# Layer one's attention started behind its gMLP, with new places for column sums, weight sums and final sums

## The chip, the cores and the metric

One core of one Trainium2 chip. The metric is device time in microseconds (us) of one execution: the median of the runs shown.

## The reference, cut to what matters

Two layers of a trunk over 512 latent and 256 context tokens, width 1024. Each layer feeds four mixers from one projection, gates each and merges them.

```
def _layer(x, xc, c, c_ctx, tabs, ...):
    h = _rms(x, norm_w) * (1.0 + sc) + sh
    aq, ak, av, az, dq, dk, dv, dz, bf, bz, cu, cv, cz = _split_in(h @ w_in)
    o_a = _attend_blocked(qa, ka, va)
    o_d = _attend_window_sink(qd, kd, vd, kd_c, vd_c, sink)
    o_b = _fourier_mix(bf, w_fnet)
    o_c = _spatial_gate(cu, cv, w_sp, b_sp)
    y = _merge(h, (o_a, o_d, o_b, o_c), (az, dz, bz, cz), w_br, w_merge, b_merge, w_out)
    return x + gt * y

def _merge(h, outs, gates, w_br, w_merge, b_merge, w_out):
    yb = stack([o * silu(z) for o, z in zip(outs, gates)])
    y = einsum('bnrw,rwd->bnrd', yb, w_br)
    g = sigmoid(h @ w_merge + b_merge).reshape(b, n, N_BRANCH, D_MODEL)
    return sum(g * y, axis=2) @ w_out
```

The context tokens go through the same layer with the same weights. Only layer one (l = 0 in the code) updates them.

## The kernel before, in words

Activations lie transposed: 128 channels on the partitions, tokens along the free dimension (256 context, then 512 latent). Everything is float32 by three products: an operand is split into a rounded part hi and the rest lo, and a product is hi·hi + hi·lo + lo·hi (`mm3` L244 to L250, `block` L811 to L818).

**Weights** come as a stream of some 170 numbered items in layer one. An item is 128x512 (256 KB) or 128x256. SP loads it into wr (L216, three raw buffers), ACT rounds it into wh (L226), DVE subtracts it into wl (L227), and TensorE (PE) uses wh twice and wl once. wh and wl have three buffers each. Each call of `wnext` (L229 to L242) takes the next item, issues loads up to 5 items ahead and the rounding and subtraction up to 3 items ahead.

**Order.** The program is written as generators that yield costs; `drive` interleaves a main one with a filler, `mix` runs a step of a side job behind each step of a main one, and `laced` runs a step of `ada_rest` each time that a number of cost units has gone by. A step of `ada_rest` is one 256 KB load and two DVE instructions (L342); the steps compute the rest of both layers' modulation. A scheduler then fixes one static order for each engine, and each engine runs its list in order.

**Layer one** goes like this. The first norm and the first part of the modulation end at about 68 us. Then come the v projection, with the rotary steps of k and q (`Rope.finish`, L548 to L581, mostly DVE) mixed in, and the gMLP's u projection (`uproj`), with the stacks mixed in: 16 transfers ks and 4 qs on SP's queue that copy k and q into the layout for scores (L603, L590). Attention of branch A and then D runs as main generator, 24 units each of scores, softmax and values (`attention` L682, paced by PACE), with a filler: gMLP (`gmlp`), q projection, z projections, merge of branch C, the Fourier branch's projections, and the first 5 of the 8 column tiles j of branch A's merge (HELD). The last 3 run behind the attention, beside the Fourier mixing (`fnet`) and the column sums (`combos`, L770 to L802): sums and differences of blocks of h, split into hi and lo (tiles T2, T3, T4 and, in `first_sum`, T1).

These sums serve the merges of D and B (`merge_s`, L829). There the gate matrix of a pair of column tiles (j, j+4) is computed by seven block products in place of eight, each 128x384 wide, with sums of weight blocks (`prep`, L172 to L177). Items that hold a sum have a 'z' buffer as raw tile. In a pair the gates are multiplied with the branch products and added to M, the sum over the branches: for D by an accumulating transfer on POOL's queue (L842), for B, the last branch (`final`), by a DVE addition (L840). Then B splits M into hi (ACT, L870) and lo (DVE, L871) for the output projection. That, the second norm and layer two follow.

Names in the rows: s scores, p probabilities, tp and pt transposed ones, o attention's output, p_cu the u projection, v_cv the gMLP's v, gl and gc gate products, yl and yc branch products, z, x and y block products, g gates, sp the spatial product.

Of the kernel before, what the change touches and what calls it, by code (L numbers as in the profile page):

```python
# [19 lines left out]
P = 128  # L20
# [6 lines left out]
PACE = (3900, 4000)  # L27
# [4 lines left out]
ADA, ADA_S = 4800, 6500  # L32
HELD = 5
# [16 lines left out]
def hybrid_trunk(tc, xt, cv, crow, win, wst, wkv, wm, wo, wada, wadat, sm, bsp, wsp, wfn, kc, krope, kmask,  # L50
# [8 lines left out]
    with ExitStack() as es:  # L59
# [93 lines left out]
        def merged_s(l, r):  # L153
# [9 lines left out]
            for j in range(4):  # L163
# [7 lines left out]
                def prep(a11=a11, a12=a12, a21=a21, a22=a22, s1=s1):  # L171
# [3 lines left out]
                    V.tensor_sub(raws[a11], t, raws[a11])  # L175
                    V.tensor_sub(raws[a12], raws[a12], raws[a11])
                    s1.append(t)  # L177
# [52 lines left out]
        def wnext():  # L230
# [249 lines left out]
        for l in range(DEPTH):  # L480
# [50 lines left out]
            class Rope:  # L531
# [16 lines left out]
                def finish(self):  # L548
# [24 lines left out]
                    V.tensor_mul(s[:, 0, L], t[:, 0, L], sin)  # L573
                    V.tensor_mul(t[:, :, L], t[:, :, L], both(cos))
                    V.tensor_add(t[:, 1, L], t[:, 1, L], s[:, 0, L])
                    V.tensor_sub(t[:, 0, L], t[:, 0, L], s[:, 1, L])
                    y = pools["m"].tile([P, 4, NT], F32R, name=f"y{name}", tag="m")
                    for i in (1, 0):
                        A.copy(y[:, i, cs], t[:, i, cs])
                        V.tensor_sub(y[:, 2 + i, cs], t[:, i, cs], y[:, i, cs].bitcast(F32))  # L580
                    return y, cs  # L581
# [141 lines left out]
            def merge(r, first=False, final=False, ctag="mm", part=range(KT)):  # L723
                yb = YB[r]
                mlp = mq = None
                for j in part:
# [3 lines left out]
                    if not last:  # L730
                        gyc = bank(f"gc{l}{r}{j}", ctag)
# [97 lines left out]
            def merge_s(r, final=False):  # L829
                for j in range(4):  # L830
# [4 lines left out]
                    def gate(i, jj, g, yd):  # L835
# [3 lines left out]
                        if final:  # L839
# [14 lines left out]
                    V.tensor_add(g1[:, H2], y, g1[:, H2])  # L854
                    yd = yield from branch(r, j, ("o", "t"))
# [8 lines left out]
                    if final:  # L864
                        if j:
                            lq = pq.tile([P, 2, NT], F32R, name=f"ML{l}{j}", tag="q")
                        for i, jj in enumerate((j, j + 4)):
                            hi = tl(("yb", "k", "p", "k")[j], f"MH{l}{jj}", F32R)
                            lo = lq[:, i, :] if j else tl("yb", f"ML{l}{jj}", F32R)
                            A.activation(hi[:, WC], M[jj][:, WC], AF.Copy, scale=0.5)  # L870
                            V.scalar_tensor_tensor(out=lo[:, WC], in0=M[jj][:, WC], scalar=0.5,  # L871
                                                   in1=hi[:, WC].bitcast(F32), op0=ALU.mult, op1=ALU.subtract)
                            MH[jj], ML[jj] = hi, lo
# [200 lines left out]
            def laced(main, other, per):  # L1074

                bal = 0
                for x in main:
                    yield x
                    bal += x or 0
                    if bal >= per:  # L1080
                        bal -= per
# [21 lines left out]
            def stacks_a():  # L1103

                TAB.clear()
                yk = yield from rk.finish()
                if l == 0:
                    yq = yield from RQ[0].finish()
# [300 lines left out]
```

## Time and profile before

| | us |
|---|---|
| median of 3 runs | 1209.08 |
| lowest and highest run | 1208.01, 1211.55 |
| profiled execution, its own time | 1206.17 |
| its span | 1204.4 |
| PE busy | 1169.6 (97%) |
| DVE busy | 794.1 (66%) |
| ACT busy | 499.6 (41%) |
| POOL busy | 14.1 (1%) |

The span is the stretch from the first to the last instruction in the trace of one execution; 1.8 us lie around it. The profiled execution is 2.9 us below the median. The page gives busy time by engine; the views of the trace give what an engine waited for, the instructions in order of time, and busy time by stretch. PE is busy nearly all the time, so that its waits are what can be saved.

### The profile page before, as it was taken

How to read it: one execution, taken by the hardware profiler on the slowest of the kernel's cores; microseconds unless marked ns; L12 is line 12 of the kernel's file. 1: busy time of each engine (PE TensorE's matmuls, PEld its weight loads, DVE VectorE, ACT ScalarE, POOL GpSimd, SP SyncE). 2: the span in 40 equal slices, each digit the busy share in tenths (PEclk: the TensorE clock that was granted, in tenths of full speed). 3: DMA queues.
4: the chain of work that ended last, by engine and by line, in shares of the span. 5: the costliest groups of instructions: out<-in, count | busy, mean ns of one | idle time of the engine just before them, and what ended most of it. 6: DMA issues, size and time to landing. Idle time of an engine off the chain costs nothing.

```text
span 1204.4 us, 18892 instructions
## 1 busy us (share of the span) xinstructions
PE 1169.6 (97%) x7068; PEld 999.9 (83%) x7068; DVE 794.1 (66%) x1688; ACT 499.6 (41%) x991; POOL 14.1 (1%) x20
## 2 busy tenths in 40 slices
PE   6999999999999999799999999999999999999998
PEld 3789788888888888799898888887888888888887
DVE  5683557767767657877786469758766676454553
ACT  5443634333333423444444256545444443333431
POOL 0000000000000000010000000000000000000000
PEclk9999999999999999999999999999999999999999
DMA  8718114222222353365432444473433223333353
GB/s 319 239 29 221 49 45 105 88 71 89 94 90 81 82 155 84 97 147 150 106 123 88 133 155 141 133 200 104 121 98 103 81 85 92 88 92 96 97 170 123
DMA packets 77099, 140.38 MB, mean 117 GB/s; under 512 B 9168, under 2 KB 19536, under 8 KB 77008
## 3 DMA queue, kind: packets, MB, share of 16 engines
q1 hardware_dynamic: 66496, 119.77, 33.4%
q10 hardware_dynamic: 8208, 13.12, 3.5%
q0 software_dynamic: 2304, 6.29, 3.0%
q8 instruction: 55, 0.90, 0.3%
q14 instruction: 36, 0.29, 0.1%
HBM read 117.13 MB, written 4.19 MB: 101 GB/s over the span
## 4 chain that ended last, share of the span: by engine, by line
PE 88%; DVE 5%; DMA 3%; ACT 2%; issue 1%; SPq 1%; ACTq 0%; DVEq 0%
PE gl L247 7%; PE gl L250 7%; PE gl L248 7%; PE o L708 4%; PE tp L675 3%; PE ow L247 3%; PE ow L248 3%; PE ow L250 3%; PE p L247 3%; PE p L248 3%; PE p L250 3%; PE yl L250 2%; PE yl L247 2%; PE yl L248 2%; PE z L815 2%; PE z L817 2%
## 5 line engine op out<-in xcount | busy, mean ns | idle before, releaser
L226 ACT CAST wh<-wr 128x512 fp32r<-128x512 f32 (+1 forms) x336 | 194.2, 579 | 376.7 <-PE gl L248 89.3
L227 DVE TENSOR_TENSOR wl<-wr,wh 128x512 fp32r<-128x512 f32 (+1 forms) x336 | 213.6, 638 | 168.9 <-ACT wh L226 167.5
L247 PE MATMUL gl<-hh,wh 128*128 128x512 f32 x384 | 154.1, 401 | 0.0
L250 PE MATMUL gl<-hh,wl 128*128 128x512 f32 x384 | 150.3, 391 | 1.7 <-DVE wl L227 1.7
L248 PE MATMUL gl<-hl,wh 128*128 128x512 f32 x384 | 149.9, 390 | 0.0
L659 ACT ACTIVATE p<-s,ng 128x768 f32<-128x768 f32 (+3 forms) x80 | 60.0, 751 | 107.3 <-DVE ng L656 58.0
L651 DVE TENSOR_REDUCE mx<-s 128x1 f32<-128x768 f32 (+3 forms) x80 | 61.5, 769 | 50.5 <-PE s L645 29.3
L250 PEld LDWEIGHTS gl<-hh,wl 128*128 128x128 f32 x384 | 72.1, 188 | 17.9 <-DVE wl L227 2.1
L342 DVE CUSTOM_DVE_ANT_0 aj<-at,cb 128x512 f32<-128x512 f32 x112 | 76.0, 686 | 16.4 <-DMA at<-in_wadat_dram 14.4
L247 PEld LDWEIGHTS gl<-hh,wh 128*128 128x128 f32 x384 | 72.3, 188 | 12.9 <-ACT g L746 0.2
L248 PEld LDWEIGHTS gl<-hl,wh 128*128 128x128 f32 x384 | 72.4, 189 | 12.6
L247 PE MATMUL p<-hh,wh 128*128 128x512 f32 (+1 forms) x192 | 71.6, 373 | 0.5 <-ACT vg L910 0.5
L247 PE MATMUL ow<-MH,wh 128*128 128x512 f32 (+1 forms) x200 | 69.4, 347 | 1.0 <-DVE ones1b L404 1.0
L250 PE MATMUL ow<-MH,wl 128*128 128x512 f32 (+1 forms) x200 | 69.4, 347 | 0.8 <-DVE wl L227 0.8
L248 PE MATMUL ow<-ML,wh 128*128 128x512 f32 (+1 forms) x200 | 69.4, 347 | 0.0
L250 PE MATMUL p<-hh,wl 128*128 128x512 f32 (+1 forms) x192 | 68.2, 355 | 0.0
L248 PE MATMUL p<-hl,wh 128*128 128x512 f32 (+1 forms) x192 | 68.2, 355 | 0.0
L708 PEld LDWEIGHTS o<-pt,vt 128*64 128x64 f32 x736 | 40.8, 136 | 16.8 <-issue 13.7
L675 PEld LDWEIGHTS tp<-kconst,p 128*128 128x128 f32 x368 | 44.6, 140 | 11.0 <-issue 0.9
L675 PE MATMUL tp<-kconst,p 128*128 128x128 f32 x368 | 53.5, 273 | 0.0
L708 PE MATMUL o<-pt,vt 128*64 128x128 f32 x736 | 52.4, 279 | 0.6 <-DVE pt L677 0.6
L677 DVE COPY pt<-tp 128x384 f32<-128x384 f32 (+1 forms) x80 | 41.9, 524 | 8.9 <-PE tp L675 8.9
(532 smaller groups left out, 2772.1 us busy)
## 6 DMA issues: line engine op xcount, KB each, us to landing
wr<-in_wm_dram SPq DMA_DIRECT2D x128, 256.0 KB, 2.7
wr<-in_win_dram SPq DMA_DIRECT2D x72, 256.0 KB, 2.8
at<-in_wadat_dram SPq DMA_DIRECT2D x64, 256.0 KB, 2.7
wr<-in_wo_dram SPq DMA_DIRECT2D x40, 256.0 KB, 2.8
aw<-in_wada_dram SPq DMA_DIRECT2D x16, 512.0 KB, 5.6
wr<-in_wm_dram SPq DMA_DIRECT2D x64, 128.0 KB, 2.2
ks<-yk SPq DMA_DIRECT2D x32, 192.0 KB, 4.4
M<-g POOLq DMA_DIRECT2D x16, 384.0 KB, 4.5
```

Source lines behind the costliest of these rows:

```text
L226: A.copy(hi[:, :n], raw)
L227: V.tensor_sub(lo[:, :n], raw, hi[:, :n].bitcast(F32))
L247: T.matmul(d, wh, xh[:, c0:c1], start=first and op, stop=False)
L248: T.matmul(d, wh, xl[:, c0:c1], start=False, stop=False)
L250: T.matmul(d, wl, xh[:, c0:c1], start=False, stop=last and cl)
L342: V.tensor_tensor_reduce(out=junk[:, :512], in0=row[i], in1=cb[v], scale=0.5, scalar=0.0, op0=ALU.mult, op1=ALU.add, accum_out=macc[j // 1 ...
L651: V.reduce_max(out=mx, in_=sv, axis=AX.X)
L659: A.activation(p[:, :nk], sv, AF.Exp, bias=ng, scale=0.125, accum_out=sm_)
L675: T.transpose(tp[:, (i - g0) * P:(i - g0 + 1) * P], p[:, i * P:(i + 1) * P], ident)
L677: V.tensor_copy(pt[:, g0 * P:g1 * P], tp[:, :(g1 - g0) * P])
L708: T.matmul(dst[64 * hx:64 * hx + 64, :], vt[kt_ // 3][:, kt_ % 3, c0:c0 + 64], pts[hx][:, j * P:(j + 1) * P], start=(j == 0), stop=(j == l ...
L815: T.matmul(dst, wh[:, q], xh, start=start and i == 0, stop=False, skip_group_check=True)
```

## The change

1. Layer one's attention starts when the gMLP is done: `uproj` takes steps of the rotary finish and stacks and no longer waits for their end ("u"), and `gmlp` takes the rest ("stk"). The v projection takes a side step only every second time, and `Rope.finish` yields in more places in layer one (fine). PACE of layer one goes from 3900 to 3600.
2. All 8 column tiles of branch A's merge belong to the filler. What is left of the filler when attention ends is the main generator, with `fnet` and `combos` as its side, unscaled. `tail` runs what is left of the side, and `first_sum`, in front of the last branch product of that merge.
3. `prep` is cut in two, prep1 and prep2, at two items; sums are made up to three items ahead, behind the splits of the items in front of them, and loads of items that have sums are issued up to 9 items ahead (AHEAD).
4. In the last block merge, pairs 0 to 2 add to M by POOL's transfers, six more than before, and their split into hi and lo (`finish`) is placed in the next pair. Pair 3 stays as it was.
5. Steps of `ada_rest` come every 3900 units until attention ends (4800 before) and every 7500 in the block merges (6500 before).

PE's matmuls are the same and of the same number. Layer two is not changed.

The diff, cut:

```
-PACE = (3900, 4000)
+PACE = (3600, 4000)
-ADA, ADA_S = 4800, 6500
-HELD = 5
+ADA, ADA_S = 3900, 7500
+AHEAD = 9
...
-                item(a12, 512)
-                item(a12, 512, prep, lambda k=a11: raws[k])
+                item(a12, 512, prep1)
+                item(a12, 512, prep2, lambda k=a11: raws[k])
...
-            wload(max(k for k, *_ in items[i:i + LOADS]))
-            wround(i + 2)
-            while prepped[0] < min(i + 3, len(items)):
+            wload(max(it[0] for n, it in enumerate(items[i:i + AHEAD]) if n < LOADS or it[2]))
+            wround(i + 3)
+            while prepped[0] < min(i + 4, len(items)):
...
-            wround(i + 3)
...
+                    if tail and j == KT - 1:
+                        tail()
                     wh, wl = wnext()
                     yield from mmp(yd, wh, wl, yb, 0, 2)
...
-                        if final:
+                        if final and j == 3:
                             V.tensor_add(M[jj][:, WC], M[jj][:, WC], g[:, WC])
                         else:
                             G.dma_start(M[jj], g, accum_op=ALU.add)
...
                     A.copy(g1[:, H2], z)
                     V.tensor_add(g1[:, H2], y, g1[:, H2])
+                    if final and j:
+                        finish(j - 1)
...
-                pre = [("v", lambda: mix(vproj("v", list(range(6)), vsink), sa, False))]
+                pre = [("v", lambda: mix(vproj("v", list(range(6)), vsink), sa, False, 2))]
...
-                pre += [("stk", lambda: mix(uproj(), sa)), ("gmlp", gmlp)]
+                pre += [("u", lambda: mix(uproj(), sa, False)), ("stk", lambda: mix(gmlp(), sa))]
...
-                ("ma", ("a0", lambda: laced(merge(R_A, part=range(own)), ada, ADA))),
+                ("ma", ("a0", lambda: laced(merge(R_A, tail=tail), ada, rate))),
...
             drive(att(), filler)
-            run(filler)
             if l == 0:
-                side = seq([("fnet", fnet), ("sums", combos)])
-                drive(paced(merge(R_A, ctag="o", part=range(own, KT)), 1.0), side)
-                run(side)
-                first_sum()
+                drive(filler, side)
```

**Three places in the engines' lists.** Line numbers in rows of the change are its own, some 2 to 24 higher than before's.

DVE behind the attention, where the column sums lie: fa and fb are sums of h's tiles, T2l, T3l and T4l parts of the sums' lo, wl a weight item's lo. Before, a stretch between two wl:

```order
L786 TENSOR_TENSOR fa_5180<-hh_1_186,hl_1_194 128x768
L227 TENSOR_TENSOR wl_5218<-wr_5144,wh_5217 128x512
L788 TENSOR_TENSOR T_5116<-fa_5180 128x384
L786 TENSOR_TENSOR fa_5224<-hh_2_187,hl_2_195 128x768
L789 TENSOR_TENSOR fa_5180<-fb_5181,fa_5180 128x384
L788 TENSOR_TENSOR T_5117<-fa_5224 128x384
L790 TENSOR_TENSOR fb_5181<-fb_5181,T_5116 128x384
L796 TENSOR_TENSOR T3l_5112<-fa_5180,T3h_5110 128x384
L791 TENSOR_TENSOR fb_5181<-fb_5181 128x384
L789 TENSOR_TENSOR fa_5224<-fb_5225,fa_5224 128x384
```

And now, the end of the first of two such stretches (28 rows lie between the wl ahead of it and the one below), in the same place of the work:

```order
L801 TENSOR_TENSOR fb_4941<-fb_4941,T_4938 128x384
L799 TENSOR_TENSOR T_4938<-fa_4984 128x384
L802 TENSOR_TENSOR fb_4941<-fb_4941 128x384
L807 TENSOR_TENSOR T2l_4930<-fb_4941,T2h_4928 128x384
L800 TENSOR_TENSOR fa_4984<-fb_4985,fa_4984 128x384
L807 TENSOR_TENSOR T3l_4934<-fa_4940,T3h_4932 128x384
L807 TENSOR_TENSOR T4l_4937<-fb_4941,T4h_4936 128x384
L801 TENSOR_TENSOR fb_4985<-fb_4985,T_4938 128x384
L807 TENSOR_TENSOR T3l_4934<-fa_4984,T3h_4932 128x384
L802 TENSOR_TENSOR fb_4985<-fb_4985 128x384
L807 TENSOR_TENSOR T2l_4930<-fb_4985,T2h_4928 128x384
L229 TENSOR_TENSOR wl_5013<-wr_4842,wh_5012 128x512
```

The sums' rows have moved from a stretch with 11 rows between two wl to two stretches with more, 28 and then, over three items, 30.

ACT in the last block merge, behind the first pair: wh is a weight item's rounding, MH the hi of the final sum, g the gates, z a block product. Before, then now:

```order
L870 ACTIVATE MH_6393<-M_2193 128x768
L861 ACTIVATE g_6200<-g_6200,bmh_683 128x768
L226 CAST wh_6411<-wr_6304 128x512
L226 CAST wh_6436<-wr_6322 128x512
L870 ACTIVATE MH_6397<-M_2890 128x768
L226 CAST wh_6454<-s_114_6406 128x512
L845 COPY g_6404<-z_6401 128x384
L848 ACTIVATE g_6404<-g_6404,bmh_683 128x384
```

```order
L885 ACTIVATE g_6248<-g_6248,bmh_683 128x768
L228 CAST wh_6434<-wr_6288 128x512
L847 ACTIVATE MH_6532<-M_2193 128x768
L228 CAST wh_6453<-wr_6290 128x512
L867 COPY g_6432<-z_6429 128x384
L228 CAST wh_6481<-s_114_6389 128x512
L847 ACTIVATE MH_6536<-M_2920 128x768
L870 ACTIVATE g_6432<-g_6432,bmh_683 128x384
L228 CAST wh_6498<-wr_6451 128x256
L872 COPY g_6433<-z_6429 128x384
```

Each MH has moved back by two to three rows, behind the next pair's first copy in the second case.

PE where attention starts: s are the first scores. Before, they stood among the gMLP's v products (the row of o is attention's):

```order
L524 MATMUL v_cv_4_1113<-wh_1116,hl_5_198 128x256
L521 MATMUL v_cv_0_1111<-wh_1173,hh_6_191 128x256
L523 MATMUL v_cv_0_1111<-wl_1174,hh_6_191 128x256
L524 MATMUL v_cv_0_1111<-wh_1173,hl_6_199 128x256
L708 MATMUL o_1320<-pt_1216,vt_0_706 64x128
```

And now:

```order
L942 MATMUL sp_1428<-wsp_1288,vg_1110 64x128 x8
L942 MATMUL sp_1438<-wsp_1288,vg_1110 64x128 x4
L640 MATMUL s_1483<-ks_975,qs_1063 128x256
L641 MATMUL s_1483<-ks_984,qs_1063 128x256
L942 MATMUL sp_1450<-wsp_1288,vg_1110 64x128 x8
L942 MATMUL sp_1460<-wsp_1288,vg_1110 64x128 x4
L653 MATMUL s_1483<-ks_975,qs_1063 128x512
L654 MATMUL s_1483<-ks_984,qs_1063 128x512
L248 MATMUL p_q_1472<-hh_0_185,wh_1362 128x512
```

The first scores have moved behind the v products and z projection of the gMLP, to its spatial product; the q projection follows them.

## Rows read from the trace of the kernel before

**Rows 1.** Page, part 1: busy time, share of span, instructions, by engine.
```profile
PE 1169.6 (97%) x7068; PEld 999.9 (83%) x7068; DVE 794.1 (66%) x1688; ACT 499.6 (41%) x991; POOL 14.1 (1%) x20
```

**Rows 2.** Waits of PE over the span: us in total, times, longest.
```profile
PE z L815 <- ACT wh L226: 5.5, 2, 3.6
PE s L631 <- ACT p L659: 2.7, 4, 1.0
PE gl L250 <- DVE wl L227: 1.7, 1, 1.7
...
PE z L815 <- ACT g L845: 1.4, 1, 1.4
PE gc L247 <- DVE g L748: 1.4, 1, 1.4
...
PE p_cu L247 <- ACT vt L885: 0.8, 1, 0.8
...
PE p_cu L247 <- ACT wh L226: 0.6, 1, 0.6
PE o L708 <- DVE pt L677: 0.6, 1, 0.6
PE p L247 <- ACT vg L910: 0.5, 1, 0.5
```

**Rows 3.** Windows: length, then PE, PEld, DVE, ACT, POOL busy (x), PEclk, DMA share, GB/s.
```profile
480.00:500.00 20.00, 13.73 (x78) 11.74 (x76) 19.59 (x37) 11.16 (x22) 1.72 (x2) 1.00 0.36 79
...
502.00:503.00 1.00, 1.00 (x4) 1.00 (x4) 0.28 (x1) 0.00 (x0) 0.00 (x0) 0.50 0.80 252
```

**Rows 4.** Timeline of PE, 498 to 506: start, duration, engine, line, operation [idle <-releaser].
```profile
500.40 0.44 PE L815 MATMUL z<-T2h,wh 128*128 128x384 f32 x1 [3.62 <-ACT wh L226]
500.69 0.34 PE L816 MATMUL z<-T2l,wh 128*128 128x384 f32 x1
...
501.42 0.52 PE L815 MATMUL z<-T2h,wh 128*128 128x384 f32 x1
501.74 0.52 PE L816 MATMUL z<-T2l,wh 128*128 128x384 f32 x1
...
505.23 0.33 PE L816 MATMUL y<-T3l,wh 128*128 128x384 f32 x1
505.40 0.33 PE L817 MATMUL y<-T3h,wl 128*128 128x384 f32 x1
```

**Rows 5.** Timeline of PE, 413 to 418: a context query of attention.
```profile
415.89 0.39 PE L631 MATMUL s<-ks,qs 128*128 128x256 f32 x1 [1.03 <-ACT p L659]
```

**Rows 6.** Groups by line and form, DVE: count | busy us, mean ns.
```profile
L796 DVE TENSOR_TENSOR T2l<-fb,T2h 128x384 fp32r<-128x384 f32 x4 | 2.2, 557 | 0.1
```

**Rows 7.** Page, part 5: costliest groups, count | busy us, mean ns.
```profile
L342 DVE CUSTOM_DVE_ANT_0 aj<-at,cb 128x512 f32<-128x512 f32 x112 | 76.0, 686 | 16.4 <-DMA at<-in_wadat_dram 14.4
```

**Rows 8.** Timeline of DVE, 625 to 640, in the final merge.
```profile
634.21 0.96 DVE L840 TENSOR_TENSOR M<-M,g 128x768 f32<-128x768 f32 x1
...
638.95 1.29 DVE L227 TENSOR_TENSOR wl<-wr,wh 128x512 fp32r<-128x512 f32 x2
```

**Rows 9.** Tile M: the accumulating transfers of the merge (durations ns).
```profile
L842 POOL DMA_DIRECT2D M<-g x8: 859/859/862, 515.2 to 575.1; - x8
...
DMA to landing us min/median/max: 3.9/4.5/5.2
```

**Rows 10.** Timeline of POOL and ACT, 515 to 525, second block merge.
```profile
518.60 0.86 POOL L842 DMA_DIRECT2D M<-g  x1 [2.58 <-DVE g L837]
...
522.10 0.62 ACT L848 ACTIVATE g<-g,bmh 128x384 f32<-128x384 f32 x1 [0.20 <-DVE g L847]
```

**Rows 11.** Timeline of SP, ACT and PE behind the stack transfers, 100 to 120.
```profile
111.61 7.51 SPq L216 DMA_DIRECT2D wr<-in_win_dram  x4
...
117.42 0.62 ACT L226 CAST wh<-wr 128x512 fp32r<-128x512 f32 x1 [1.22 <-DMA wr<-in_win_dram]
...
119.38 0.28 PE L521 MATMUL v_cv<-wh,hh 128*128 128x256 f32 x1
```

More of the change, by code (lines that the diff above doesn't have):

```diff
@@ L546, in take, with finish @@
                                         op0=ALU.mult)
-                def finish(self):
+                def finish(self, fine=False):
                     cs, name = self.cs, self.name
@@ L721, in hybrid_trunk, with merge @@
             MH, ML = [None] * KT, [None] * KT
-            def merge(r, first=False, final=False, ctag="mm", part=range(KT)):
+            def merge(r, first=False, final=False, ctag="mm", tail=None):
                 yb = YB[r]
                 mlp = mq = None
-                for j in part:
+                for j in range(KT):
                     g_l = bank(f"gl{l}{r}{j}")
@@ L730, in merge @@
                     if not last:
-                        gyc = bank(f"gc{l}{r}{j}", ctag)
+                        gyc = bank(f"gc{l}{r}{j}", "o" if "a1" in flags else ctag)
                         gd.append((gyc[:, :NC], 0, NC, True, False))
@@ L829, in merge_s, with finish @@
             def merge_s(r, final=False):
+                def finish(j):
+                    if j:
+                        lq = pq.tile([P, 2, NT], F32R, name=f"ML{l}{j}", tag="q")
+                    for i, jj in enumerate((j, j + 4)):
+                        hi = tl(("yb", "k", "p", "k")[j], f"MH{l}{jj}", F32R)
+                        lo = lq[:, i, :] if j else tl("yb", f"ML{l}{jj}", F32R)
+                        A.activation(hi[:, WC], M[jj][:, WC], AF.Copy, scale=0.5)
+                        V.scalar_tensor_tensor(out=lo[:, WC], in0=M[jj][:, WC], scalar=0.5,
+                                               in1=hi[:, WC].bitcast(F32), op0=ALU.mult, op1=ALU.subtract)
+                        MH[jj], ML[jj] = hi, lo
                 for j in range(4):
@@ L863, in merge_s @@
                     gate(1, j + 4, g1, yd)
[L864 to L873, printed above, removed]
+                    if final and j == 3:
+                        finish(j)
             KS, Q = {0: [], 1: []}, {0: [], 1: []}
@@ L1079, in laced @@
                     bal += x or 0
-                    if bal >= per:
-                        bal -= per
+                    p = per[0] if "a1" not in flags else per[1]
+                    if bal >= p:
+                        bal -= p
                         next(other, None)
@@ L1105, in stacks_a @@
                 TAB.clear()
-                yk = yield from rk.finish()
+                yk = yield from rk.finish(l == 0)
                 if l == 0:
-                    yq = yield from RQ[0].finish()
+                    yq = yield from RQ[0].finish(True)
                 while ("u" if l else "v") not in flags:
@@ L1135, in hybrid_trunk, with tail @@
                 ada = ada_rest([(1, j) for j in range(16, 24)], 1)
-            own = HELD if l == 0 else KT
+            if l == 0:
+                side = seq([("fnet", fnet), ("sums", combos)])
+                def tail():
+                    run(side)
+                    first_sum()
+            else:
+                tail = None
             filler = seq(pre + [
                 ("q1", lambda: qblock(1)), ("z0", lambda: mix(zblock(0), sd)),
-                ("mc", lambda: laced(merge(R_C, first=True), ada, ADA)), ("z1", lambda: laced(zblock(1), ada, ADA)),
-                ("b", lambda: laced(bproj(), ada, ADA)),
-                ("ma", ("a0", lambda: laced(merge(R_A, part=range(own)), ada, ADA))),
+                ("mc", lambda: laced(merge(R_C, first=True), ada, rate)), ("z1", lambda: laced(zblock(1), ada, rate)),
+                ("b", lambda: laced(bproj(), ada, rate)),
+                ("ma", ("a0", lambda: laced(merge(R_A, tail=tail), ada, rate))),
             ])
-            pace = PACE[l]
+            pace, rate = PACE[l], (ADA, ADA_S)
             def att():
```

20 lines of the change are left out of this document (15 added, 5 removed).

## The prediction

> **What bounds the kernel now.** First the page: PE is busy 1169.6 of 1204.4 us [rows 1], so everything that any rearrangement can win lies in the other 34.8. Then the view of PE's waits [rows 2]. It tells what ended each wait, and the reader is to see that no single one is large: the rows are a list of short waits, nine kinds in layer one, 15.2 us in all. Two groups are in the first part: four waits of scores for the previous probabilities (2.7), two of the u projection (0.8 and 0.6), one each of attention's output (0.6) and of a projection for the gMLP (0.5). The others lie around the column sums and in the block merges: 1.7 and 1.4 for DVE's rows of branch A's merge, 5.5 in two for a rounded weight, 1.4 for a gate copy. Third, the windows [rows 3]: from 480 to 500 us DVE is busy 19.59 of 20 us and PE only 13.73, so there DVE is the bound. Fourth, PE's timeline behind it [rows 4]: after the wait of 3.62 us matmuls of 384 columns start every 0.32 us (501.42, 501.74), and at 505.23 and 505.40 every 0.17. The granted clock is 0.50 between [rows 3], the lower level of 1.2 GHz. It lasts for some 12 matmuls, 501.4 to 505.0, and so costs about 12 x 0.15 = 1.8 us. With it the most that the change can reach is 15.2 + 1.8 = 17 us.
>
> **The change, part by part**, as gains (+) and losses (-) of time.
>
> *Rotary finish spread over more steps.* The u projection's second weight stands behind a long row of DVE work, and its bank waits for ACT. With the finer steps the weight's lo is due in between: both waits go, +1.4 [rows 2]. What is late next is the weight behind the 20 stack transfers: SP's queue comes to it at 111.61, and it is rounded at 117.42 [rows 11]. Before, attention's first units lay ahead of its use, 1.8 us of matmuls (three scores of 0.7 and 0.4 for transposes, less what now lies there too) and 1.4 of waits that are gone. So PE wants it 3.2 us earlier than 119.38, the first use before [rows 11], at 116.2, and with rounding it is there at 118.0. If SP's transfers start no earlier, the loss is 1.8; the key's part is now finished before the query's and lets SP start sooner, which makes it nothing. I take the middle, -0.9, and keep 0 to -1.8.
>
> *Attention behind the gMLP.* Its first units no longer share ACT with GELU, whose table loads stand between the exponentials. Of the waits there, output and projection (0.6 + 0.5) and two of the four of scores go: +2.1. The other two are context queries, the 1.03 of [rows 5] and one like it of 0.66: a short unit that follows another after only 1.85 us of PE's work. In the new order at least 3.8 us lie between: +1.7. Against it, the rotary finish of the second query, some 12 us of DVE between two weights, now lies among full units with 768 keys. The trace has no such place; bounds are nothing and three waits as long as the longest of scores, 1.0 [rows 2]. I take one: -1.0. The spatial product, for which scores are now queued in front, waits for a bank that DVE releases behind a weight: nothing to -1.0, nearest to the 0.5 for a projection [rows 2]; -0.5.
>
> *Column sums right behind attention.* This is the largest loss. In DVE's new list 28 rows and one weight's lo lie between the last Fourier product and the third item behind it. Of these 13 are 128x384 of 0.56 [rows 6], three are 128x768 of 0.96 [rows 8], the rest are ten short ones, two of 0.42, and the weight. That is 14.2 us, 11.5 with the 0.09 by which neighbours overlap (two weights take 1.29 and not 1.38, [rows 8]). PE has matmuls for 8.5 us in that stretch, counted in its list at the pitch of 0.17 us for 384 columns [rows 4], others by their columns. Over the next three items it is 15 of 128x384, three of 128x768, four steps of the modulation of 0.69 [rows 7], and weights and gates: 16.9, less overlap 14.4, against 11.0 of PE. PE waits 3.0 and 3.4, with a little for latencies 6.6. The waits of 1.7 and 1.4 that the same work costs now [rows 2] end: -3.5. Bounds: no more than now (0), and without overlap (-8.4). I take the middle value since DVE's rows between 480 and 500 run that closely [rows 3].
>
> *Sums three items ahead, first pair of the block merges.* The wait of 3.62 [rows 4] is for sums whose last load waits for a buffer, then lands, is summed four times and rounded. Loading and two sums come earlier now, the buffer does not: 2.7 are left, +0.9 (0 to +3.6).
>
> *Last block merge.* Two waits, 1.9 (5.5 less 3.6) and 1.4 [rows 2], follow runs of DVE of seven and more us in which additions to M and splits of 0.96 [rows 8] stand ahead of weights. Six additions leave DVE, some 14 steps of the modulation go to earlier places, and splits and weight sums alternate with the weights: +3.3. The price is a new wait: ACT's MH now needs a transfer's landing, and rounded weights and copies of the next pair are queued behind it. The template is the merge before: the second transfer is issued at 518.60 [rows 10], lands 3.9 to 5.2 later [rows 9], at 522.5 to 523.8, and ACT's gate, which is now behind MH, starts at 522.10 there. With MH's own 0.9 ACT falls back 1.3 to 2.6 us. Three weight buffers of 12 matmuls each are 2 x 12 x 0.17 = 4.1 us ahead at this place, less 1.2 for rounding and lo: PE does not see it. I take off 0.3 and keep 0 to -1: +3.0. POOL, with 14.1 us of work in all, is not a bound.
>
> Of these transfers the Trainium skill (SBUF — State Buffer, "SBUF: two separate sides") has a rule against the change: their descriptors are written by GpSimd, which a DVE instruction with the shared port locks out, so that a short transfer took five times as long. Here no run shows that: POOL's eight issues take 859 to 862 ns each beside a busy DVE [rows 9]. By the row the part gives +3.0; what the rule would make of it is the third rival.
>
> *Each wait* also costs at its end: the first matmuls start 0.29 apart and not 0.17 [rows 4]. Some ten go and three come: 7 x 0.12 = +0.8. *The clock* falls once before and, I assume, once after: 0.
>
> *Sum:* 1.4 - 0.9 + 2.1 + 1.7 - 1.0 - 0.5 - 3.5 + 0.9 + 3.0 + 0.8 = +4.0. The span becomes 1200.4 and the profiled execution 1202.2. That execution is 2.9 below the median of 1209.1, so the forecast for the median is **1205.1 us**.
>
> **The rivals.** (A) *The column sums cost no more than they do now.* If weights are far enough ahead when the Fourier products end, DVE's excess of 3.0 and 3.4 is mostly taken by the lead. For it speaks that a full DVE cost only 3.1 in the present place, against it that the new stretch puts 26 us of DVE beside 19.5 of PE. That gives back 3.5, and without a wait as long as 3.6 the clock does not fall: 1.8 more. 1205.1 - 5.3 = 1199.8.
>
> (B) *They cost the clock too.* Both new waits come near the 3.62 behind which the clock fell. Two more falls: 1205.1 + 3.6 = 1208.7, no change.
>
> (C) *The transfers land late,* the slower side. Place: MH in the last merge's pairs 1 to 3. An accumulating transfer beside DVE's uninterrupted run (as the additions and weights of [rows 8] are part of) waits for it. From a landing of about 8 us on (5.2 and the 2.9 of lead) each pair stalls by the excess; at 11 us, three pairs by 3 us: 1205.1 + 9 = 1214. It makes the change slower than before from 9.4 us on. Against it speaks that no transfer of M landed later than 5.2 [rows 9]. The Trainium skill's rule, above, would do just this.
>
> (D) *The start of attention does not get better.* It is only moved: the waits for probabilities and tables come back at the new place (2.1 and 1.7 not won, two more waits of 1.0). 1205.1 + 5.8 = 1210.9.
>
> **How the numbers follow.** A measurement of this kernel tells 0.3%, 3.6 us, from no change; the line is 1205.5. Chances: forecast 0.42, A 0.22, B 0.16, C 0.08, D 0.12. The forecast's own range is 1202 to 1208.5, with a little more than half under the line. Faster: 0.24 + 0.22 + a little of B, 0.48. Slower, over 1212.7: most of C and a third of D and the worst of the column sums, 0.16. No change: 0.36. The range from 1199 to 1211.5 leaves out C and the ends of A and D.
>
> **What would show it.** In the changed kernel's profile the waits of u projection, scores behind probabilities and gates in the last merge are gone from PE's list; the wait for lo behind DVE's column sums is there twice with 3 us or so, each at DVE over 95% busy; the first block product still waits 2 to 3 us; MH on ACT shows a wait for the transfer of 1 to 2 us that nothing on PE answers to. I am wrong if PE waits less than 3 us around the column sums (A), if the granted clock falls more than once behind 400 us (B), if matmuls of the last merge wait for weights rounded behind MH (C), or if the attention's first ten units show waits over 3 us in all (D).

## The result, and the profile after

| | median us | lowest and highest | ratio to before |
|---|---|---|---|
| before | 1208.93 (4 runs) | 1208.01, 1211.55 | |
| the change | 1200.13 (4 runs) | 1198.33, 1201.62 | 0.9923 (0.9901 to 0.9945) |

The change makes the kernel 0.8% faster, 8.8 us by the medians, where 4.0 were forecast. The forecast of 1205.1 us is 5 us too slow; the time lies in the stated range, near its lower end. Its profiled execution took 1201.11 us, with a span of 1199.3.

First the waits of PE (us in total, times, longest), now a shorter list around the change, some rows left out:

```profile
PE gl L251 <- DVE wl L229: 4.0, 2, 3.5
PE z L826 <- DVE wr L179: 3.2, 1, 3.2
...
PE n1b L412 <- DVE nq1b L391: 1.4, 1, 1.4
...
PE yl L248 <- ACT g L757: 0.6, 1, 0.6
PE gcs L995 <- DMA kd<-in_kdft_dram: 0.6, 1, 0.6
PE z L826 <- ACT g L872: 0.3, 2, 0.2
...
PE v_cv L524 <- DVE wl L229: 0.2, 1, 0.2
```

Against [rows 2]: scores behind probabilities (2.7), the u projection's two waits (0.8 and 0.6), attention's output (0.6) and the gMLP's projection (0.5) are gone. Of the block merges' waits the two late ones are gone but for 0.3, the wait of the first block product is 3.2 and not 3.6, and DVE's column sums cost 4.0 and 0.6 where they cost 1.7 and 1.4. The wait of n1b, in the second norm behind layer one, is not the change's alone: it is 0.8, 1.0 and 0.3 in three kernels below (e4, e3, e10) that hold only parts of it.

Then the windows around the sums and the first block product (length, then PE, PEld, DVE, ACT, POOL busy (x), PEclk, DMA share, GB/s), to be read against [rows 3]:

```profile
440.00:445.00 5.00, 2.24 (x10) 1.50 (x8) 5.00 (x11) 2.81 (x6) 0.00 (x0) 0.93 0.11 41
445.00:452.00 7.00, 6.25 (x22) 5.12 (x23) 6.69 (x15) 1.74 (x4) 0.86 (x1) 0.57 0.58 142
...
496.00:503.00 7.00, 6.58 (x22) 6.57 (x23) 4.47 (x10) 2.21 (x5) 0.00 (x0) 0.55 0.27 79
```

The granted clock lies at 0.57 and 0.55 in two stretches of 7 us. Window by window it is 0.50 from 445 to 451 and from 496 to 502, the lower level of 1.2 GHz (the half clock, below), and it fell while PE waited. Before, there was one such stretch of some 3.4 us [rows 3, 4].

PE's timeline of the same place (start, duration, engine, line, operation [idle <-releaser]) and DVE's beside it:

```profile
441.85 0.39 PE L249 MATMUL gl<-hl,wh 128*128 128x512 f32 x1
445.75 0.80 PE L251 MATMUL gl<-hh,wl 128*128 128x512 f32 x1 [3.51 <-DVE wl L229]
446.34 0.63 PE L248 MATMUL gl<-hh,wh 128*128 128x512 f32 x1
446.77 0.63 PE L249 MATMUL gl<-hl,wh 128*128 128x512 f32 x1
```

```profile
432.97 0.68 DVE L229 TENSOR_TENSOR wl<-wr,wh 128x512 fp32r<-128x512 f32 x1
...
443.61 0.55 DVE L807 TENSOR_TENSOR T3l<-fa,T3h 128x384 fp32r<-128x384 f32 x1
444.08 0.55 DVE L802 TENSOR_TENSOR fb<-fb 128x384 f32<-128x384 f32 x1
444.55 0.55 DVE L807 TENSOR_TENSOR T2l<-fb,T2h 128x384 fp32r<-128x384 f32 x1
445.01 0.68 DVE L229 TENSOR_TENSOR wl<-wr,wh 128x512 fp32r<-128x512 f32 x1
```

DVE runs without a pause from 433.94 to 446; between the two wl (432.97 and 445.01) lie just the 28 rows that the changed list showed, and PE, which needs the second, stands from 442.2 to 445.75. Behind it, matmuls of 512 columns start 0.43 to 0.59 apart, 0.23 being usual.

Third, ACT's timeline in the last block merge, behind a transfer that POOL issued at 590.67, and then the tile M with its groups of issues and landings:

```profile
595.62 0.85 ACT L847 ACTIVATE MH<-M 128x768 fp32r<-128x768 f32 x1 [1.77 <-DMA M<-g]
596.37 0.60 ACT L870 ACTIVATE g<-g,bmh 128x384 f32<-128x384 f32 x1
...
597.18 0.47 ACT L872 COPY g<-z 128x384 f32<-128x384 f32 x1
```

```profile
L864 POOL DMA_DIRECT2D M<-g x14: 859/860/862, 511.9 to 629.2; - x14
...
DMA to landing us min/median/max: 3.9/4.7/5.8
```

MH stands behind the transfer for 1.77 us (0.75 to 1.77 in the six places; forecast 1 to 2). The landing row is of all transfers of M; the 14 of the block merges took 3.9 to 5.7, the six new ones 3.9 to 4.9. All that PE shows of it is the 0.3 of z behind ACT's copy.

### The profile page after: what moved, and what is told of

It reads as the page before. It is cut to its first block, busy times and chain, and to the rows that moved or that the text cites. A ratio compares the mean times of both kernels' runs of the same rounds, so it can differ in the third digit from the quotient of the medians.

```text
span 1199.3 us, 18917 instructions
## 1 busy us (share of the span) xinstructions
PE 1168.8 (97%) x7068; PEld 1002.9 (84%) x7068; DVE 788.2 (66%) x1682; ACT 495.7 (41%) x987; POOL 19.3 (2%) x26
## 4 chain that ended last, share of the span: by engine, by line
PE 81%; DMA 8%; DVE 7%; issue 2%; ACT 1%; SPq 1%; ACTq 0%; DVEq 0%; POOLq 0%
PE gl L248 7%; PE gl L251 7%; PE gl L249 7%; PE o L717 4%; PE tp L684 3%; PE ow L248 3%; PE ow L249 3%; PE ow L251 3%; PE p L248 2%; PE yl L251 2%; PE yl L248 2%; PE yl L249 2%; PE p L251 2%; PE p L249 2%; DMA at<-in_wadat_dram 2%
## 5 line engine op out<-in xcount | busy, mean ns | idle before, releaser
L686 DVE COPY pt<-tp 128x384 f32<-128x384 f32 (+1 forms) x80 | 41.9, 523 | 10.1 <-PE tp L684 9.7
```

The source lines that it names most:

```text
L686: V.tensor_copy(pt[:, g0 * P:g1 * P], tp[:, :(g1 - g0) * P])
```

## The experiments

All ratios are to the kernel before, in runs on the same chip, with 95% intervals. Three batches of four ran; before's median was 1208.07, 1207.85 and 1208.63 us in them. Where a kernel is said to be faster or slower than before by some us, it is the ratio's distance from 1 times 1208. One kernel against another goes by the medians; the change ran in a batch of its own, in which before was 1208.93, so that against the change the ratios give up to 2 us less of a gain.

### The kernel before, again (e1_before)

No edit.

> The kernel before, once more. Its recorded execution took 1206.2 us, its timed runs 1208.0 to 1211.6. Theory: the same waits, 1208.5 to 1209.5 us; the waits around the column sums and in front of the first block product come out a little longer than in the recorded execution, and the half clock (granted 0.50) lasts some 7 us behind them and not 3.4, which is 1.8 us more. Rival: no more half clock than in the record; then the 2.7 us between record and runs lie in waits elsewhere, or in no place that the views show.

Measured: 1208.11 us (1206.81 to 1210.82, 11 runs), ratio 1.0000 (0.9991 to 1.0008). Behind 66 us the waits of 0.8 us and more are those of [rows 2], but the half clock is found in a second place, behind the u projection's two waits. PE's timeline and the window there:

```profile
88.05 0.38 PE L247 MATMUL p_cu<-hh,wh 128*128 128x256 f32 x1 [0.84 <-ACT vt L885]
...
89.11 0.50 PE L247 MATMUL p_cu<-hh,wh 128*128 128x512 f32 x1 [0.56 <-ACT wh L226]
...
91.09 0.63 PE L250 MATMUL p_cu<-hh,wl 128*128 128x512 f32 x1
91.51 0.63 PE L247 MATMUL p_cu<-hh,wh 128*128 128x512 f32 x1
```

```profile
91.00:92.00 1.00, 1.00 (x4) 0.72 (x3) 1.00 (x2) 0.00 (x0) 0.00 (x0) 0.50 0.99 368
```

From 90 to 93.6 matmuls of 512 columns start 0.43 us apart. The same stretch stands in the run of the last merge alone (e3_final, 88 to 92) and in that of e11_behind (90 to 93). It is not in the execution that the prediction was made from, nor in that of e4_sums:

```profile
88.00:93.00 5.00, 4.94 (x25) 4.00 (x26) 5.00 (x8) 1.85 (x4) 0.00 (x0) 1.00 0.98 276
```

Two short waits of 0.84 and 0.56, with 0.5 us of work between, are so followed by the half clock in three executions of five that have them. The half clock behind the first block product is there in both, 3.4 us long, so the expectation of a longer one failed. In these 11 runs the clock does not sort the times: those with a mean clock of 0.999 took 1207.9 to 1209.4, those with 0.997 1206.8 to 1209.0. Over the 66 runs of this kernel in the three batches it does in part: 18 with 0.999 took 1207.3 us on average, 33 with 0.997 took 1208.5, and each of the two groups spreads over 4 us.

### The attention part alone (e2_attention)

```
-PACE = (3900, 4000)
+PACE = (3600, 4000)
...
-                pre = [("v", lambda: mix(vproj("v", list(range(6)), vsink), sa, False))]
+                pre = [("v", lambda: mix(vproj("v", list(range(6)), vsink), sa, False, 2))]
...
-                pre += [("stk", lambda: mix(uproj(), sa)), ("gmlp", gmlp)]
+                pre += [("u", lambda: mix(uproj(), sa, False)), ("stk", lambda: mix(gmlp(), sa))]
```

and the finer steps of `Rope.finish`, all on the kernel before.

> Only the attention part of the change on the kernel before: rotary finish in finer steps, start behind the gMLP, pace 3600. Theory (waits end one by one): the waits of the u projection (1.4 us), of output, projection and scores at attention's start (2.1) and of the two context queries (1.7) are gone, 0.3 comes back at the gMLP's v, column sums and merges stay as before: 5 to 6 us faster, about 1203.5. Rival (the parts help each other): the column sums, which then meet another place in attention's end, take 2 us or more of it back: 1205 or more.

Measured: 1197.50 us (1196.99 to 1198.22, 4 runs), ratio 0.9909 (0.9895 to 0.9922). This part alone is 11 us faster than before, twice what was expected. Its median is 2.6 below that of the whole change, with overlapping intervals. PE's waits in layer one are now, but for 0.3 of attention's output, only those of the sums and merges, unchanged:

```profile
PE z L823 <- ACT wh L226: 5.5, 2, 3.6
...
PE gl L250 <- DVE wl L227: 1.7, 1, 1.7
PE z L823 <- ACT g L853: 1.4, 1, 1.4
PE gc L247 <- DVE g L756: 1.4, 1, 1.4
```

Where the 9.8 us between the spans of e1 and e2 (1205.0 and 1195.2) lie can be read from the starts of the same matmuls: the first of the u projection (p_cu) and the first of the gMLP's v (v_cv), in e1 and then in e2.

```profile
86.57 0.40 PE L247 MATMUL p_cu<-hh,wh 128*128 128x512 f32 x1
107.09 0.28 PE L521 MATMUL v_cv<-wh,hh 128*128 128x256 f32 x1
```

```profile
86.03 0.40 PE L247 MATMUL p_cu<-hh,wh 128*128 128x512 f32 x1
102.75 0.28 PE L521 MATMUL v_cv<-wh,hh 128*128 128x256 f32 x1
```

- Up to the v projection e2 gets 0.5 us ahead, where no edit lies, and keeps this up to the u projection.
- The 96 matmuls of the u projection take 20.5 us in e1 and 16.7 in e2. Before and e4_sums, which have its two waits without the half clock, take 18.9 each. So the two waits of 1.4 cost 2.2 with their ends, and the half clock 1.6.
- From v_cv to the first z it is 387.9 us in e1 and 381.6 in e2, 6.3 less. Nearly all of it lies in attention's own matmuls: s, tp and o, from each start to the next, take 78.0 and 71.9. Of the 6.3, 2.6 are waits in the list. What sets the other 3.7 stays open.
- Behind the first z, where no edit lies, 0.8 are lost again.

### Its two halves (e10_fine, e11_behind)

e10_fine: the finer steps of `Rope.finish` and

```
-                pre = [("v", lambda: mix(vproj("v", list(range(6)), vsink), sa, False))]
+                pre = [("v", lambda: mix(vproj("v", list(range(6)), vsink), sa, False, 2))]
```

> Only the finer steps of the rotary finish (and a side step behind every second step of the v projection) on the kernel before; attention starts where it did. Theory: the two waits of the u projection (1.4 us) go, and the half clock of 3.4 us that follows them in some executions (1.8 us) with them: 2 to 3.5 us faster, 1204.5 to 1206. Rival: the wait only moves to the weight behind the stack transfers; less than 1 us faster.

Measured: 1204.73 us (1201.58 to 1208.04, 12 runs), ratio 0.9974 (0.9963 to 0.9985). The u projection's waits are gone, and no half clock stands before 500 us: the theory. In the traces the u projection takes 16.7 us, 3.8 less than in e1, and from v_cv to the first z nothing changes (387.9 both). How much of the 3.1 is the clock's is not shown by the runs: their mean clock is 0.9975, that of the 17 runs of before beside them 0.9974.

e11_behind: the order alone.

```
-                pre += [("stk", lambda: mix(uproj(), sa)), ("gmlp", gmlp)]
+                pre += [("u", lambda: mix(uproj(), sa, False)), ("stk", lambda: mix(gmlp(), sa))]
```

> Only the start of attention behind the gMLP on the kernel before; the rotary finish and the pace stay as they were. Theory: the waits at attention's start (2.1 us) and of the two context queries (1.7) go, those of the u projection and the half clock behind stay: 4 to 7 us faster, 1201 to 1204; with the finer steps it makes up the 10.6 us of the attention part. Rival: the order counts for less than the waits that end, and most of the 10.6 us needs both together: 2 us or less faster.

Measured: 1203.81 us (1202.56 to 1204.05, 5 runs), ratio 0.9960 (0.9947 to 0.9972). All four waits of scores are gone, and with them those of output and projection; the u projection keeps its 0.84 and 0.56 and the half clock behind. So the context queries' waits did end with the new order and not with the pace. From v_cv to the first z it takes 382.7 us, 5.2 less than e1. The halves make 3.1 and 4.8, 7.9 of the 11; in the traces, from the u projection to the first z, 3.8 and 5.2 of the 10.1 of e2. What the rest needs, the pace of 3600 or both together, was not tried.

### The last block merge alone (e3_final)

```
-                        if final:
+                        if final and j == 3:
                             V.tensor_add(M[jj][:, WC], M[jj][:, WC], g[:, WC])
...
                     V.tensor_add(g1[:, H2], y, g1[:, H2])
+                    if final and j:
+                        finish(j - 1)
```

> Only the last block merge of the change on the kernel before: additions to M by transfers in pairs 0 to 2, splits in the next pair. Theory: two of the three waits of that merge go (1.4 and 1.9 us), no new one comes, since landing takes 3.9 to 5.8 us and ACT's MH waits 1 to 2 us beside weights that are far enough ahead: 3 to 4 us faster, about 1205.5. Rival (transfers late): MH holds up the rounded weights, PE waits in three pairs: no faster, 1208 or more. Second rival: without the weight sums' new places a part of the waits stays: 1 to 2 us faster.

Measured: 1206.28 us (1204.52 to 1208.26, 11 runs), ratio 0.9981 (0.9972 to 0.9990): 2.3 us faster, between the theory and its second rival. PE's waits of 1.9 and 1.4 are gone, and two of 1.1 together have come:

```profile
PE z L815 <- ACT wh L226: 3.6, 1, 3.6
...
PE z L815 <- ACT g L861: 1.1, 2, 0.6
```

It is the new wait that the prediction priced at 0.3. ACT's timeline at its second place shows how it comes about:

```profile
601.20 0.85 ACT L836 ACTIVATE MH<-M 128x768 fp32r<-128x768 f32 x1 [2.50 <-DMA M<-g]
...
602.75 0.47 ACT L861 COPY g<-z 128x384 f32<-128x384 f32 x1
603.12 0.62 ACT L226 CAST wh<-wr 128x512 fp32r<-128x512 f32 x1
```

MH waits 2.50 us for the transfer, and the copy of z behind it ends at 603.2; PE, which needs z's bank for the next product, has been idle for almost 0.6 by then. A transfer's landing so does reach PE, by a copy and not by the rounded weights, and by 0.6 in a pair, not by 3.

### The column sums' place alone (e4_sums)

```
-                for j in part:
+                for j in range(KT):
...
+                    if tail and j == KT - 1:
+                        tail()
...
             drive(att(), filler)
-            run(filler)
             if l == 0:
-                side = seq([("fnet", fnet), ("sums", combos)])
-                drive(paced(merge(R_A, ctag="o", part=range(own, KT)), 1.0), side)
-                run(side)
-                first_sum()
+                drive(filler, side)
```

> Only the new place of the column sums on the kernel before: all of branch A's merge in the filler, the sums right behind attention. Theory: DVE has runs of 17 and 6 us between two weights' lo there, so the wait on PE is longer than in the changed kernel (some 5 to 8 us in place of 3.1), with one or two half clocks of 7 us, and the wait for the first block product is 3: slower by 3 to 6 us, 1212 to 1215. Rival: the place itself brings the gain (weights ahead, first block product not held up): 1 to 3 us faster.

Measured: 1211.39 us (1210.23 to 1215.64, 11 runs), ratio 1.0032 (1.0022 to 1.0042): slower by 3.9. The waits that grew:

```profile
PE gl L246 <- ACT g L747: 5.2, 1, 5.2
PE z L816 <- DVE wr L175: 3.3, 1, 3.3
```

ACT's gates, which must empty the banks, come late:

```profile
455.45 0.47 ACT L747 ACTIVATE g<-gc,bmh 128x256 f32<-128x256 f32 x1 [7.75 <-DVE macc L341]
455.87 0.51 ACT L796 CAST T2h<-fb 128x384 fp32r<-128x384 f32 x1
456.29 0.68 ACT L747 ACTIVATE g<-gl,bmh 128x512 f32<-128x512 f32 x1
```

The first has stood for 7.75 us behind DVE, which runs without a pause from 449.63 on, and one rounding of the sums lies between it and the second, for which PE waits. The granted clock is 0.50 for 6 us behind each of PE's two waits. So this part of the change loses time, by its waits and by the clock.

### The change without it, without the weight sums' order, and with the old rates (e8_oldsums, e9_oldprep, e12_ada)

e8_oldsums is the change with the edit of e4_sums undone.

> The change without its new place for the column sums: the last three column tiles of branch A's merge stand behind attention again, with the sums beside them. Theory (the parts add): the attention part gave 10.6, the last merge 1.8, the sums' place lost 3.3, so this is about 3 us faster than the change, 1196 to 1198, with waits of 1.7, 1.4 and 3.6 at the sums and one half clock of 3.4 us. Rival (the sums' place pays in company with the other parts): slower than the change, 1201 or more.

Measured: 1196.45 us (1195.10 to 1199.80, 6 runs), ratio 0.9909 (0.9893 to 0.9926). The waits are the expected ones (1.7, 1.4, and 3.7), the half clock one of 3.4 us. The median is the expected one, 3.7 below the change (1.7 by the ratios); the two intervals overlap (0.9901 to 0.9945 for the change), so that the loss of the sums' place stands on e4_sums.

e9_oldprep is the change with this undone:

```
-                item(a12, 512, prep1)
-                item(a12, 512, prep2, lambda k=a11: raws[k])
+                item(a12, 512)
+                item(a12, 512, prep, lambda k=a11: raws[k])
...
-            wload(max(it[0] for n, it in enumerate(items[i:i + AHEAD]) if n < LOADS or it[2]))
-            wround(i + 3)
-            while prepped[0] < min(i + 4, len(items)):
+            wload(max(k for k, *_ in items[i:i + LOADS]))
+            wround(i + 2)
+            while prepped[0] < min(i + 3, len(items)):
...
+            wround(i + 3)
```

> The change with the weight blocks' sums as before: in one piece, made right before their first item, no loads ahead. Theory: in the last merge a wait or two comes back (up to 2 us, as in the run of the last merge alone, which kept 1.1 us behind ACT's copies), the first block product waits 3.2 to 3.6 as it does now: 0 to 2.5 us slower than the change. Rival: DVE has room in those merges, so nothing changes, within 0.5 us.

Measured: 1201.85 us (1200.59 to 1202.96, 6 runs), ratio 0.9945 (0.9932 to 0.9958). The median lies 1.7 above the change (2.7 by the ratios), the intervals overlap, and no wait of the merges came back: the first block product waits 3.1, and the last merge 0.2. A gain of this part is not shown.

e12_ada is the change with `ADA, ADA_S = 4800, 6500`.

> The change with the steps of the modulation at their old rates, 4800 and 6500. Theory: DVE has less to do beside the column sums (four steps of 0.69 us fewer in the second run), and more in the last merge; the sums' second wait (1.1 us) goes, the first (3.5) stays: within 1 us of the change, rather faster. Rival: the steps in the last merge bring its waits back: 1 to 3 us slower.

Measured: 1199.51 us (1198.17 to 1201.21, 6 runs), ratio 0.9926 (0.9914 to 0.9938): no difference to the change. Inside, a wait of 1.4 is back in the last merge and 3.9 stands at the sums.

### The sums spread, the weight block's buffer, and both (e5_spread, e6_raw, e7_both)

e5_spread, on the change:

```
-                drive(filler, side)
+                drive(paced(filler, 0.6), side)
```

> The change, with the column sums and Fourier steps spread: behind attention the costs of branch A's merge count 0.6, so that the side job takes about 1.7 times as much of PE's work. DVE's longest run between two weights' lo falls from some 12 us to some 6. Theory (the crowding of DVE there is what costs): the waits of 3.5, 0.5 and 0.6 us around the sums and the half clock of 6.8 us behind the first of them (2.6 us) go, those of the first block product (3.2) and the half clock behind it stay: 5 to 7 us faster than the change, about 1194. Rival (the sums cost DVE the same wherever they lie): the waits are only cut in smaller pieces, less than 2 us faster.

Measured: 1190.94 us (1189.54 to 1193.11, 4 runs), ratio 0.9861 (0.9844 to 0.9878), 9.2 us below the change by the medians, 7.5 by the ratios, whose intervals do not overlap. The windows around the sums:

```profile
440.00:460.00 20.00, 20.00 (x117) 17.68 (x116) 19.44 (x44) 9.57 (x19) 1.72 (x2) 1.00 0.58 145
460.00:480.00 20.00, 20.00 (x116) 17.37 (x115) 15.52 (x36) 8.88 (x17) 1.72 (x2) 1.00 0.52 126
```

From 440 to 460 DVE is as busy as in the change (19.44 and 19.55 us), but PE now is 20.00 (15.89 in the change) and its clock 1.00 (0.83). So what cost time was not the amount of DVE's work but the 28 rows between two weights. The longest time from one wl to the next beside the sums, which was 12.0 us, now is 7.0:

```profile
432.61 0.69 DVE L229 TENSOR_TENSOR wl<-wr,wh 128x512 fp32r<-128x512 f32 x1
439.59 0.69 DVE L229 TENSOR_TENSOR wl<-wr,wh 128x512 fp32r<-128x512 f32 x1
```

Up to the output projection this execution is 8.9 us ahead of the change's. Of this 4.6 are waits; 2.7 are the half clock behind them, which is gone (half of 5.3 us of work); and 1.2 the one at the first block product, which is 3.4 us long here and not 6.8, though the wait in front of it (3.2) is the same. Against it stands a wait of 1.7 us for the Fourier matrix kd, which was 0.6. That makes 7.4; where the other 1.5 come from is not shown.

e6_raw, on the change:

```
-                return (wm[l, r, j, :, 512 * h:512 * h + 512], 512, "wraw" if h and j < 4 else "z")
+                return (wm[l, r, j, :, 512 * h:512 * h + 512], 512,
+                        "wraw" if h and j < 4 else "p" if h and j == 4 and r == R_D else "z")
```

with `wload` taking the tile from the pool that is named.

> The change, with the one weight block of the first pair that its first sum waits for (wr86) in a buffer of the pool p in place of z, where it had to wait for the split of the Fourier branch's output. Theory: its load is issued some items earlier, the wait of 3.2 us in front of the first block product goes to under 1 us, and with it the half clock behind (2.8 us): 4 to 6 us faster than the change. Rival: the load is then held by another buffer or by SP's queue, and the wait stays: within 1 us of the change.

Measured: 1195.75 us (1192.85 to 1202.52, 6 runs), ratio 0.9904 (0.9881 to 0.9926). The wait in front of the first block product is gone from PE's list. The profiled execution, the slowest of the six (1202.52), has another in its place:

```profile
PE gl L252 <- DVE wl L230: 4.0, 2, 3.5
...
PE gcs L996 <- DMA kd<-in_kdft_dram: 2.6, 1, 2.6
```

The Fourier matrix kd lands only when it is needed, in the change and in its variants with the sums' new place: this wait is 0.6 to 2.6 us there, and before has none. Here a half clock came with it, and another at 48 us, in the modulation; layer one's v projection starts 2.7 us later than in the change. From the first z to the output projection this execution takes 151.6 us, the change 157.5. The median is 4.4 below the change (2.3 by the ratios), with overlapping intervals: the mechanism is shown, the gain is not separated from noise.

e7_both is the two edits together.

> Spread sums and the other buffer together. Theory: both gains add, no half clock is left behind 400 us: 9 to 12 us faster than the change, about 1190, and faster than the attention part alone. Rival: the spread sums end later and hold up the first block product, so that the second gain is lost: 1194 or more.

Measured: 1189.07 us (1186.12 to 1190.43, 4 runs), ratio 0.9841 (0.9822 to 0.9859), the fastest of all, 19 us below before and 11 below the change (10 by the ratios). From e5_spread it isn't told apart. Its windows between 440 and 500:

```profile
440.00:460.00 20.00, 20.00 (x116) 17.64 (x115) 19.44 (x44) 9.57 (x20) 1.72 (x2) 1.00 0.58 146
460.00:480.00 20.00, 19.52 (x111) 16.81 (x110) 16.42 (x37) 7.98 (x16) 1.72 (x2) 1.00 0.54 139
480.00:500.00 20.00, 19.92 (x117) 19.08 (x116) 13.68 (x29) 10.03 (x19) 0.86 (x1) 1.00 0.46 119
```

PE idles 0.6 us in these 60, and no half clock is left until the last microsecond of the kernel.

## Why the prediction was right in the sign and short in the size

*The sum as a whole.* By the parts run alone, 11.0 (attention), 2.3 (last merge) and -3.9 (column sums) make 9.4, and the change has 9.3 by its ratio, each of the two sums known to 2 or 3 us: the parts add up within that. In the forecast attention and rotary finish stood with 2.8, so this part gave 8 more than forecast, and the rest about 3 less. That the time lies in the stated range at all is in part luck: two errors of opposite sign. It also lies at the time of rival A, 1199.8, whose condition did not come.

*The base of the sum.* For the profiled execution 1202.2 was forecast and 1201.11 measured, 1.1 off. The median was then taken to lie 2.9 above the profiled execution, as before; now it lies 1.0 below. Executions of before go from 1205.43 to 1211.55, and the one that the sum started from, 1206.17, was the sixth fastest of 71. The clock sorts this spread only in part (above). Another part lies in layer two, which no edit touches: from the output projection to the end the 14 traces take 549.1 to 553.0 us, the change's being the longest. What sets it is open. Stretch by stretch the two profiled executions differ by -0.2 up to the u projection, +2.2 in it, +3.7 from there to the first product of the Fourier branch (p_bf), -2.1 to the first z, +3.8 to the output projection and -2.3 behind it: 7.4 were won in layer one, and 5.1 are left.

*Rotary finish.* Forecast +1.4 and -0.9 for the weight behind the stack transfers. The two waits went. Of the -0.9 there is 0.2 [v_cv in the list above]: SP came to that weight at 108.54 and not at 111.61 [rows 11], as the lower bound had it. What the step left out is that the ends of the two waits cost 0.8 more (forecast: 0.12 a wait), and the half clock of 1.6 us that follows them in three traces of five: e10_fine measured 3.1 for a step that stood with 0.5. The trace that the prediction was made from happened to be an execution without it, and the sum had the clock at 0.

*Attention behind the gMLP.* Forecast +2.1 and +1.7, and -1.0 and -0.5 against them. Both gains came, the losses did not: no unit waits for the second query's rotary finish, and none for the spatial product's bank. Together with the rotary finish it was forecast at 2.8 and measured at 11. **This is the term that failed**: 2.2 of the difference are the three losses, which were put at -2.4 and came to -0.2. Between the traces of e1 and e2 another 2.4 are the u projection's clock and ends of waits, and 3.7 the steps between attention's matmuls that no view of waits shows and that the forecast put at nothing beyond 0.12 for each wait.

*Column sums.* Forecast waits of 3.0 and 3.4, and 6.6 with a little more, from rows of DVE's new list with their durations and overlaps. Measured 3.5 for the first; of the second 1.1, probably since PE lay further behind by then, as the half clock had slowed it; no run separates this. The term was -3.5; by waits it is 4.6 - 3.1 = -1.5. To it come two stretches of half clock of nearly 7 us in place of one of 3.4: PE worked 5.3 and 5.9 us at the lower clock, and 3.4 before, which costs 3.9 more. e4_sums measured -3.9 for the place alone. The size is right, but for another reason in part: "the clock falls once before and, I assume, once after: 0" is the second step that failed. It fell twice after, each time for twice as long. That is rival B's sign, and at 3.9 nearly its price (3.6); that the change is faster even so is attention's gain. Nor does the clock need a wait as long as 3.6, as rival A had it: it fell behind 3.2 here, and behind the 0.84 and 0.56 of the u projection in e1.

*First block product.* Forecast 2.7 left of 3.6; it is 3.2, and e9_oldprep has 3.1 without the earlier sums, so that these brought nothing here. The buffer was the cause, as the step said; e6_raw shows it.

*Last block merge.* Forecast +3.0; waits of 3.7 in all went and 0.3 came, 2.3 us measured alone. MH's wait was forecast by the landing of the merge before and came so. Rival C, the late transfer, fell: the 14 transfers landed in 3.9 to 5.7 us, against the 8 from which it would begin to decide, and POOL's 14 issues took 859 to 862 ns each while DVE was 69% busy (82.0 of 119 us, from 511 to 630). The Trainium skill's rule (SBUF — State Buffer, "SBUF: two separate sides"), by which a DVE instruction with the shared port keeps GpSimd from writing the descriptors of such transfers, is not seen in this trace. The trace is no test of it, though: the same section ties the rule to modes that `copy`, `cast` and `tensor_scalar` can enter and `tensor_tensor` has not, and none of the first three is among DVE's operations from 511 to 630.

Rival A fell, since the sums did cost more than before, and D fell, since attention's waits did not come back at the new place.

## What to carry to other kernels

A side job on an engine that feeds the bottleneck costs by its longest run between two operands more than by its sum: with 17.2 us from one weight's lo to the next (e4_sums) PE waited 5.2 us there, with 12.0 (the change) 3.5, and with 7.0 (e5_spread) not at all. Spreading the same rows over more of PE's work took 7 to 9 us off. Price a wait with what follows it: here each of the 17 waits of over 3 us around the sums and block merges, in 13 of the 14 traces, was followed by 3.4 or 6.8 us at half clock, which cost up to half of that time more. And one trace is one execution; before a sum is made of small terms, a second trace shows which of them come and go.

## What was not expected of the hardware

The half clock lasted two lengths, about 3.4 us (before, e2, e5, e8) and 6.8 us (the change, e4, e9), and the wait in front does not tell which. Behind the same wait of 3.6 us in front of the first block product it was 3.4 us long in five executions (before, e1, e2, e3, e10) and 6.8 in e11; behind one of 3.2 it was 6.8 in the change and 3.4 in e5 and e12. In the u projection the same 96 matmuls with the same two waits had it behind them in three executions (e1, e3, e11) and not in two (before, e4). And the mean clock of a run tells only part of its time: runs of before at the same mean clock differ by 4 us.
